# Pacing the context's chain: more of it beside block 1's feed-forward, fewer steps beside the causal attention

## The chip, the cores and the metric

The kernel runs on one core of one Trainium2 chip. The metric is the device time of one execution in microseconds (us). Its engines are TensorE (PE; PEld is its weight load), VectorE (DVE), ScalarE (ACT), GpSimd (POOL) and SyncE (SP), which issues most of the DMAs.

## What is computed

Two blocks of two layers each on 256 tokens of width 1024. The first has an RWKV time mix, a dense feed-forward, a causal attention ("moba": with 256 tokens there is one block of keys, so it is plain causal attention with 16 heads of 64) and a mixture of eight experts. The second works on the result x and on a context of its own, 256 tokens that don't depend on the first block.

```python
def first_block(x, ...):
    h = deepnorm_residual(x, rwkv7_time_mix(x), ln_g[0, 0], ln_b[0, 0])
    h = deepnorm_residual(h, swiglu(h), ln_g[0, 1], ln_b[0, 1])
    h = deepnorm_residual(h, moba_attention(h), ln_g[1, 0], ln_b[1, 0])
    return deepnorm_residual(h, moe_swiglu(h), ln_g[1, 1], ln_b[1, 1])

def second_block(x, ctx):                      # layer 0, the context's side:
    hc = modulate(rms_norm(xc, norm_g[0, 0]), csh1, csc1)
    yx, yc = even_mixer(hx, hc, ...)           # attention | bidirectional mLSTM, then w_out
    xc = xc + cg1 * rms_norm(yc, norm_g[0, 1])
    hc = modulate(rms_norm(xc, norm_g[0, 2]), csh2, csc2)
    xc = xc + cg2 * rms_norm(conv_ffn(hc, ...), norm_g[0, 3])
```

## The kernel before

All matrix products with large weights are made from float32 numbers split in two parts of a shorter format: each weight tile of 128 x 1024 is loaded by SP's queue (`wload`, L363) into one of six buffers `wraw`, copied by ACT into its high part `whi` (L303, pieces of 512 columns) and subtracted by DVE into its low part `wlo` (L306), with four buffers each. A product then takes three matmuls: high times high, low times high, high times low (L318). Transposes are matmuls too (L338). PSUM is two pools of four banks, `ps(0)` and `ps(1)`, for two chains of work.

Block 1's parts are generators, and so is the context's side of the second block, `ctx_even`. A step of a generator ends at a `yield`. `rated` runs a main chain and, after each of its steps, as many steps of the side chain as are due: a main step that yields nothing adds `rate`, one that yields a number adds that number, and the whole part of the sum is run. `block1_front` does this for four parts with the rates `A_RATES`: the time mix's output projection (`rwkv_out`), the feed-forward (`ffn_dense`), the causal attention (`moba`) and the router (`moe_route`). Within `moba`, `paced` lets the steps of the input projections yield `SIDE["moba_in"]` = 0, those of the softmax pipeline `SIDE["moba"]`, and those of the output projection `SIDE["moba_out"]` = 0; its first step (transposes of h) and its last (the norm) take the rate. What is still left of the side chain is run at the end.

Steps of the main chains: `rwkv_out` 5 (four of `lin_tok`, one of the norm); `ffn_dense` 36 (one of transposes; parts of 12 and 10 hidden tiles with 12 and 10 steps of up and gate products and six of the down projection each; one of the norm); `moba` one, then its input projections, ten of the softmax pipeline (eight pairs of heads: in step i the scores of pair i, the values of pair i - 2, the transposes of pair i - 1, the softmax of pair i), its output projection, and one of the norm.

Steps of `ctx_even`: one of the first norm, 15 of `even_proj`, 12 of `mlstm`, ten of `attend` (eight half pairs, pipelined in the same way; the first also finishes the mLSTM's output), four of `lin_tok` within `out_proj` (columns 0 to 511 by two halves of the depth, then columns 512 to 1023, both halves, by two halves of the tokens; the third also makes the gate's row), one of the residual, and one of the second norm (`modulated`, with 16 transposes and their splits).

The generators give the program order. A list scheduler of the language then puts each engine's instructions in order: program order is the priority, and of what is ready by its own model of time the earliest in the program goes first, so that a later instruction can slip ahead where an engine would be free.

Of the kernel before, what the change touches and what calls it, by code (L numbers as in the profile page):

```python
# [634 lines left out]

ADA_EVERY = 10
WKV_END = 286
A_RATES = (1.0, 0.8, 1.0, 0.0)
WKV_AR = 3
WKV_T = ((2.3, 1.0), (0.6, 1.7), (0.0, 1.0))  # L640
WKV_PC = (1, 0, 0)
# [348 lines left out]
def pipelined(n, scores, soft, turn, values):  # L990

    for i in range(n + 2):
        if i < n:
            scores(i)
        if i >= 2:
            values(i - 2)
        if 1 <= i <= n:
            turn(i - 1)
        if i < n:
            soft(i)  # L1000
        yield
# [31 lines left out]
def moba(N, st, ch=0):  # L1033
# [8 lines left out]
    def keep(dst):  # L1042
        def evac(c0, nt, p):
            k = c0 // P
            N.act(dst[:, k * T:(k + nt) * T].rearrange("p (n t) -> p n t", n=nt), p)
        return evac

    def vevac(c0, ncol, tb, p):
        N.act(v[:, tb * D + c0:tb * D + c0 + ncol], p[:, :ncol])
    yield from paced(chain(N.lin_T(ch, x, KD, a["moba_w_q"], D, keep(qT)), N.lin_T(ch, x, KD, a["moba_w_k"], D, keep(kT)),  # L1050
                           N.lin_tok(ch, x, KD, a["moba_w_v"], D, vevac)), SIDE["moba_in"])
    o = N.act_slots(2, 3, "oT")
# [40 lines left out]

    yield from paced(pipelined(8, scores, soft, turn, values), SIDE["moba"])

    def evac(c0, ncol, tb, p):
        q = h[:, tb * D + c0:tb * D + c0 + ncol]
        N.stt(q, q, ALPHA, p[:, :ncol], ALU.mult, ALU.add)
    yield from paced(N.lin_tok(ch, o, KD, a["moba_w_o"], D, evac, late=lambda: None), SIDE["moba_out"])
    N.layer_norm(lambda tb: h[:, tb * D:(tb + 1) * D], (1, 0), lambda tb: h[:, tb * D:(tb + 1) * D])  # L1100
# [487 lines left out]
def attend(N, ch, o, npr, nkb, score, vsrc, scale, biased, ch2=None):  # L1588

    nc = N.nc  # L1590
    ch2 = ch if ch2 is None else ch2
    nk = nkb * P
    sc, S, R, po = {}, {}, {}, {}

    def scores(i):
        sc[i] = [N.ps(ch) for _ in range(2)]
        for hh in range(2):
            score(i // 2, hh, i % 2, sc[i][hh])

    def soft(i):  # L1600
        S[i] = [N.t512("S")[:, :nk] for _ in range(2)]
        for hh in range(2):
            p, s = sc[i][hh][:, :nk], S[i][hh]
            if biased is not None:
                biased(i // 2, hh, i % 2, p, s)
                softmax_part(N, s, s, 1.0)
            else:
                softmax_part(N, s, p, scale)
        sc.pop(i)

    def turn(i):
        R[i] = turned(N, ch2, S.pop(i), nkb)

    def values(i):
        pr, qt = i // 2, i % 2
        if qt == 0:
            po[pr] = N.ps(ch2)
        for b in range(nkb):
            for hh in range(2):
                q = slice(hh * 64, hh * 64 + 64)  # L1620
                N.mm(po[pr][q, qt * P:(qt + 1) * P], vsrc(pr, hh, b), R[i][hh][:, b * P:(b + 1) * P], b == 0, b == nkb - 1)
        R.pop(i)
        if qt:
            out_split(N, o, pr, po.pop(pr))

    yield from pipelined(2 * npr, scores, soft, turn, values)
# [208 lines left out]
def mlstm_out(N, st, ch, E, o):  # L1835

    nc = N.nc
    hs = E["kh"][:, 1024:2048]
    og = E["qo"][:, 1024:2048]
    g = N.row_load(N.a["ev_ml_norm_g_2"][0])  # L1840
    N.tt(hs, hs, og, ALU.mult)
    h3 = hs.rearrange("p (n x) -> p n x", n=8)
    mu = N.sm(8, "mu")
    nc.vector.tensor_reduce(mu, h3, axis=AX.X, op=ALU.add)
    N.ts(mu, mu, 1.0 / 128)
    N.tt(h3, h3, bc(mu, 2, 128), ALU.subtract)
    N.act(og, hs, AF.Square)
    vr = N.sm(8, "vr")
    nc.vector.tensor_reduce(vr, og.rearrange("p (n x) -> p n x", n=8), axis=AX.X, op=ALU.add)
    rs = N.sm(8, "rs")  # L1850
    N.rpow(rs, vr, 8, 1.0 / 128, 1e-6)
    N.tt(h3, h3, bc(rs, 2, 128), ALU.mult)
    h2 = hs.rearrange("p (b x) -> p b x", b=2)
    N.tt(h2, h2, bc(g[:, :512], 1, 2), ALU.mult)
    for k in range(0, 4, 2):
        p = N.ps(ch)
        for i in range(2):
            for tb in range(2):
                N.tr(p[:, i * T + tb * P:i * T + (tb + 1) * P], h2[:, tb, (k + i) * P:(k + i + 1) * P])
        N.split(o.h[:, (4 + k) * T:(6 + k) * T], o.l[:, (4 + k) * T:(6 + k) * T], p)  # L1860
# [24 lines left out]
def even_x(N, st, ch, x, S):  # L1885
    nc, a, c = N.nc, N.a, N.c
    yield from even_proj(N, st, ch, x, S, "Ex")
    E, Ec = st["Ex"], st["Ec"]
    yield from paced(mlstm(N, st, ch, E, st["CT"], st["ms"], True), SIDE["mlstm"])

# [7 lines left out]
    mlstm_out(N, st, ch, E, o)  # L1898
    yield 8 * SIDE["bias"]
    qo, kv, kvc = E["qo"], E["kv"], Ec["kv"]  # L1900
# [12 lines left out]
    def biased(pr, hh, qt, p, S_):  # L1913
        h = 2 * pr + hh
        N.stt(S_[:, 0:T], p[:, 0:T], 0.125, bias[qt][:, h * T:(h + 1) * T], ALU.mult, ALU.add)
        N.act(S_[:, T:2 * T], p[:, T:2 * T], AF.Copy, scale=0.125)
    yield from paced(attend(N, ch, o, 4, 4, score, vsrc, 0.125, biased, ch2=1 - ch), SIDE["na"])
    st["yx_act"] = o
# [164 lines left out]
def ctx_even(N, st, ch=1):  # L2083

    a, nc = N.a, N.nc
    xc = N.slot(7, "xc")
    nc.scalar.dma_start(xc.rearrange("p (b c) -> p b c", b=2), a["ctx_2"][0].rearrange("(b p) c -> p b c", p=P))
    x = modulated(N, st, ch, xc, 0, 0, 1, (12, 13), N.slot(1, "cscr"))
    yield
    yield from even_ctx(N, st, ch, x, dict(qo=1, kv=11, ml=8, kh=9, h=(12, 13)))  # L2090
    yield from out_proj(N, st, ch, st["yc_act"], a["ev_w_out_2"], xc, 0, 1, 1)
    st["xc"] = xc
    st["cffn"] = modulated(N, st, ch, xc, 0, 1, 1, (8, 9), N.slot(1, "cscr2"))
    yield
# [8 lines left out]
    yield from mla_ctx(N, st, ch, x, (10, 11), 1, 9)  # L2103


SIDE = dict(moba_in=0, moba=1, moba_out=0, start=5, mlstm=1.25, bias=0.5, na=0.5, res0=3, end0=5, mla=1.5)


def x_chain(N, st, out, ch=0):
# [24 lines left out]
def chain(*gens):  # L2134
    for g in gens:
        yield from g
# [7 lines left out]
def paced(g, n):  # L2144
    for _ in g:
        yield n


def rated(main, side, rate):

    due = 0.0
    for n in main:
        due += rate if n is None else n
        advance(side, int(due))
        due -= int(due)


def block1_front(N, st):
# [8 lines left out]
    side = ctx_even(N, st)  # L2167
    for g, r in zip((rwkv_out, ffn_dense, moba, moe_route), A_RATES):
        rated(g(N, st), side, r)
# [26 lines left out]
```

## Time and profile before

| | us |
|---|---|
| median of 3 runs | 2859.82 |
| lowest, highest | 2858.45, 2868.52 |
| the profiled execution | 2855.15 |
| its span, first to last instruction | 2853.3 |
| TensorE busy in the span | 2756.7 |
| VectorE busy | 2209.9 |
| ScalarE busy | 1775.3 |
| GpSimd busy | 68.8 |

Matmuls are pipelined and their ends are modelled: two that follow each other overlap in the rows, so what one costs is read from the distance of the starts. Busy times are unions. A name such as `ps<-whi,ych` gives what is written and what is read, without buffer numbers. The names by which the chains are told apart: `h1T` the feed-forward's input, `hid` its hidden tiles, `h2T` the input of the causal attention, `kTm`, `qT` and `vm` its keys, queries and values, `oTh` and `oTl` its output; `nq_mlo` and `nk_nav` the context's queries, keys and values, `ych` and `ycl` its attention's output, which the context's output projection reads, `xc` the context, `cscr` its second norm. Both attentions write `S` and `R`; the causal one has 384 columns, or rows of 128 and 256, the context's 256. `consts` in the sum of S is the causal mask, `diag,consts` the gate's row.

### The profile page before, as it was taken

Reading aid. Unit: us, or ns where it says so; the run is one execution under the profiler, and the core shown is the slowest. Engines: PE = TensorE matmul, PEld = TensorE weight load, DVE = VectorE, ACT = ScalarE, POOL = GpSimd, SP = SyncE. Lnnn points to the kernel's source line nnn. Section 1 sums busy time; section 2 is a strip of 40 time slices with the busy share of each in tenths; the row PEclk is TensorE's granted clock in tenths of the full one; section 3 lists DMA queues with packets and bytes.
Section 4 is the critical chain, followed back from the end, with each engine's and each line's share of the span. In section 5 each row is a group of like instructions: output and inputs, shape, how many; then the busy total and the mean of one; then the engine's idle time right before and its main releaser. Section 6 shows DMA issues by size and latency. Waiting matters only on the chain. (4 is left out here: it accounts for less than half of the span.)

```text
span 2853.3 us, 49934 instructions
## 1 busy us (share of the span) xinstructions
PE 2756.7 (97%) x18356; PEld 2265.0 (79%) x18356; DVE 2209.9 (77%) x4350; ACT 1775.3 (62%) x3603; POOL 68.8 (2%) x87
## 2 busy tenths in 40 slices
PE   8999899999999999999999999999989999999898
PEld 8677589897866787778777777778877899877897
DVE  7356385577577989998998899987688787876767
ACT  5223265444566787787878878766547665666654
POOL 0011100000000000000000000000000000000000
PEclk9999999999999999999999999999999999999999
DMA  7444655544428999999999999975543455421453
GB/s 253 155 146 153 219 195 179 179 142 132 158 94 322 362 335 345 354 358 330 350 361 342 347 347 363 352 274 178 162 131 125 138 195 178 151 80 43 148 186 125
DMA packets 183663, 641.16 MB, mean 225 GB/s; under 512 B 22737, under 2 KB 28241, under 8 KB 183410
## 3 DMA queue, kind: packets, MB, share of 16 engines
q1 hardware_dynamic: 175200, 625.58, 63.2%
q10 hardware_dynamic: 8210, 12.30, 1.4%
q8 instruction: 146, 2.39, 0.3%
q14 instruction: 107, 0.88, 0.1%
HBM read 636.76 MB, written 1.05 MB: 224 GB/s over the span
## 5 line engine op out<-in xcount | busy, mean ns | idle before, releaser
L306 DVE TENSOR_TENSOR wlo<-wraw,whi 128x512 fp32r<-128x512 f32 (+1 forms) x2181 | 1375.8, 685 | 311.4 <-ACT whi L303 249.9
L303 ACT ACTIVATE whi<-wraw 128x512 fp32r<-128x512 f32 (+1 forms) x2181 | 1214.2, 621 | 408.9 <-PE ps L318 322.0
L318 PE MATMUL ps<-whi,xg 128*128 128x512 f32 x1792 | 497.4, 397 | 1.6 <-ACT whi L303 1.6
L318 PEld LDWEIGHTS ps<-whi,xg 128*128 128x128 f32 x1792 | 327.3, 188 | 83.6 <-ACT whi L303 23.3
L318 PE MATMUL ps<-wlo,xg 128*128 128x512 f32 x896 | 294.9, 400 | 0.4
L318 PE MATMUL ps<-whi,hT 128*128 128x512 f32 x896 | 260.2, 400 | 0.0
L318 PE MATMUL ps<-hT0h,whi 128*128 128x256 f32 (+2 forms) x872 | 216.2, 286 | 4.0 <-ACT whi L303 3.5
L318 PE MATMUL ps<-hT0l,whi 128*128 128x256 f32 (+2 forms) x872 | 216.1, 285 | 0.1
L318 PEld LDWEIGHTS ps<-wlo,xg 128*128 128x128 f32 x896 | 168.4, 188 | 54.1 <-DVE wlo L306 18.6
L318 PE MATMUL ps<-whi,hid 128*128 128x512 f32 x704 | 189.9, 405 | 9.9 <-DVE cv L315 6.7
L318 PEld LDWEIGHTS ps<-whi,hT 128*128 128x128 f32 x896 | 164.8, 189 | 31.8
L318 PEld LDWEIGHTS ps<-hT0h,whi 128*128 128x128 f32 (+2 forms) x872 | 167.8, 193 | 5.3 <-ACT whi L303 3.9
L318 PEld LDWEIGHTS ps<-hT0l,whi 128*128 128x128 f32 (+2 forms) x872 | 168.0, 193 | 0.9 <-DVE hT0l L306 0.4
L318 PE MATMUL ps<-wlo,hT 128*128 128x512 f32 x448 | 168.2, 415 | 0.0
L318 PEld LDWEIGHTS ps<-whi,hid 128*128 128x128 f32 x704 | 131.7, 191 | 43.3 <-issue 14.1
L315 DVE SCALAR_TENSOR_TENSOR cv<-ps,vecs,cv 128x255 f32<-128x255 f32 x264 | 124.3, 479 | 12.3 <-ACT cv L303 11.0
L318 PE MATMUL ps<-hT1h,whi 128*128 128x256 f32 (+1 forms) x504 | 128.6, 292 | 1.7 <-ACT whi L303 1.7
L318 PE MATMUL ps<-hT0h,wlo 128*128 128x256 f32 (+2 forms) x872 | 125.9, 285 | 1.8 <-DVE wlo L306 1.6
L318 PE MATMUL ps<-hT1l,whi 128*128 128x256 f32 (+1 forms) x504 | 126.5, 287 | 0.0
L318 PEld LDWEIGHTS ps<-hT0h,wlo 128*128 128x128 f32 (+2 forms) x872 | 114.1, 192 | 3.8 <-DVE wlo L306 3.1
L318 PEld LDWEIGHTS ps<-wlo,hT 128*128 128x128 f32 x448 | 84.3, 188 | 30.5 <-DVE wlo L306 14.1
L318 PEld LDWEIGHTS ps<-hT1h,whi 128*128 128x128 f32 (+1 forms) x504 | 97.2, 193 | 4.0 <-ACT whi L303 2.6
(528 smaller groups left out, 4480.5 us busy)
## 6 DMA issues: line engine op xcount, KB each, us to landing
wraw<-moe_w_down SPq DMA_DIRECT2D x224, 512.0 KB, 5.6
wraw<-moe_w_gate SPq DMA_DIRECT2D x222, 512.0 KB, 5.2
wraw<-moe_w_up SPq DMA_DIRECT2D x222, 512.0 KB, 5.4
wraw<-ffn_up SPq DMA_DIRECT2D x132, 512.0 KB, 3.7
wraw<-ada_w SPq DMA_DIRECT2D x96, 512.0 KB, 4.6
wraw<-ffn_down SPq DMA_DIRECT2D x66, 512.0 KB, 3.7
wraw<-ffn_w_gate SPq DMA_DIRECT2D x22, 512.0 KB, 4.0
wraw<-ffn_w_up SPq DMA_DIRECT2D x22, 512.0 KB, 3.6
```

Source lines behind the costliest of these rows:

```text
L303: self.nc.scalar.activation(out, in_, f, **kw)
L306: (eng or self.nc.vector).tensor_tensor(out, x, y, op=op)
L315: (eng or self.nc.vector).scalar_tensor_tensor(out, x, s, y, op0=op0, op1=op1)
L318: self.nc.tensor.matmul(out, l, r, start=start, stop=stop)
```

## The change

Two numbers. The rate of the side chain in the feed-forward goes from 0.8 to 1.0 steps a main step, and the pace in the causal attention's softmax pipeline from 1 to 0.75. No instruction is added or removed; the place of the context's steps in the program order changes, from the feed-forward's first main step on.

```diff
-A_RATES = (1.0, 0.8, 1.0, 0.0)
+A_RATES = (1.0, 1.0, 1.0, 0.0)
...
-SIDE = dict(moba_in=0, moba=1, moba_out=0, start=5, mlstm=1.25, bias=0.5, na=0.5, res0=3, end0=5, mla=1.5)
+SIDE = dict(moba_in=0, moba=0.75, moba_out=0, start=5, mlstm=1.25, bias=0.5, na=0.5, res0=3, end0=5, mla=1.5)
```

## Rows read from the trace of the kernel before

**Rows 1.** Busy us of each engine (and instructions) in four stretches, clock, DMA share, GB/s:
```profile
660.00:684.00 24.00, 23.75 (x125) 16.15 (x123) 19.60 (x55) 13.16 (x36) 0.00 (x0) 1.00 0.50 166
...
684.00:700.00 16.00, 10.96 (x53) 8.02 (x54) 14.58 (x35) 5.79 (x16) 2.96 (x2) 0.79 0.45 148
...
766.00:828.00 62.00, 56.74 (x330) 39.00 (x329) 46.73 (x157) 45.62 (x148) 0.00 (x0) 0.97 0.21 68
...
828.00:852.00 24.00, 22.97 (x109) 18.61 (x108) 21.84 (x48) 14.55 (x34) 3.50 (x5) 1.00 0.40 132
```

**Rows 2.** Timeline (start us, duration us, engine, line, operation): the context's chain, 660 to 793 us:
```profile
660.44 0.70 PE L318 MATMUL ps<-nk_nav,nq_mlo 64*128 64x256 f32 x4
...
698.11 0.47 ACT L303 ACTIVATE S<-ps,mx 128x256 f32<-128x256 f32 x1
...
767.07 0.66 PE L318 MATMUL ps<-R,nk_nav 128*64 128x128 f32 x8
...
792.05 0.77 PE L318 MATMUL ps<-whi,ych 128*128 128x512 f32 x1
```

**Rows 3.** TensorE's groups, 766 to 828.5 us: busy us, mean ns, idle before:
```profile
L318 PE MATMUL ps<-whi,ych 128*128 128x512 f32 x32 | 13.8, 430 | 0.0
...
L318 PE MATMUL ps<-diag,consts 128*128 128x512 f32 x4 | 1.9, 592 | 0.0
...
L318 PE MATMUL ps<-R,nk_nav 128*64 128x128 f32 x32 | 3.1, 285 | 0.0
...
L318 PE MATMUL ps<-nk_nav,nq_mlo 64*128 64x256 f32 x4 | 1.0, 428 | 0.0
...
L338 PE MATMUL ps<-ident,S 128*128 128x128 f32 x60 | 11.5, 299 | 4.7 <-DVE S L310 4.4 <-ACT ych L303 0.2
```

**Rows 4.** Timeline of TensorE: two starts of the context's output projection:
```profile
801.91 0.40 PE L318 MATMUL ps<-whi,ych 128*128 128x512 f32 x1
...
802.38 0.40 PE L318 MATMUL ps<-whi,ych 128*128 128x512 f32 x1
```

**Rows 5.** Timeline of TensorE at the first norm; waits stand in brackets:
```profile
684.23 0.44 PE L338 MATMUL ps<-ident,S 128*128 128x128 f32 x2 [0.47 <-ACT R L303]
...
690.68 0.44 PE L338 MATMUL ps<-ident,h 128*128 128x128 f32 x2 [1.03 <-DVE h L315]
...
694.75 1.54 PE L338 MATMUL ps<-ident,h 128*128 128x128 f32 x6 [2.97 <-DVE h L315]
```

**Rows 6.** Windows of 2 us; the granted clock is the third column from the right:
```profile
692.00:694.00 2.00, 0.00 (x0) 0.00 (x0) 1.86 (x5) 0.00 (x0) 1.45 (x1) 0.64 0.00 0
...
698.00:700.00 2.00, 2.00 (x14) 2.00 (x13) 1.65 (x6) 0.90 (x4) 0.00 (x0) 0.65 0.36 141
...
792.00:794.00 2.00, 2.00 (x7) 1.63 (x8) 0.75 (x4) 0.93 (x4) 0.00 (x0) 0.50 0.04 8
```

**Rows 7.** Window of the causal attention with hardly any neighbour, 782 to 792 us:
```profile
782.00:792.00 10.00, 5.88 (x35) 3.32 (x35) 6.95 (x28) 6.19 (x23) 0.00 (x0) 0.98 0.00 0
```

**Rows 8.** Timeline: starts of causal softmaxes, their transposes, the last output copy:
```profile
767.17 0.42 DVE L306 TENSOR_TENSOR S<-ps,consts 128x256 f32<-128x256 f32 x1
...
779.96 0.42 DVE L306 TENSOR_TENSOR S<-ps,consts 128x256 f32<-128x256 f32 x1
...
785.52 0.75 DVE L306 TENSOR_TENSOR S<-ps,consts 128x256 f32<-128x256 f32 x2
...
791.07 0.61 PE L338 MATMUL ps<-ident,S 128*128 128x128 f32 x3 [1.33 <-DVE S L310]
...
791.98 0.42 DVE L306 TENSOR_TENSOR S<-ps,consts 128x256 f32<-128x256 f32 x1
...
827.97 0.39 ACT L303 ACTIVATE oTh<-ps 128x256 fp32r<-128x256 f32 x1
```

**Rows 9.** VectorE's largest group, 828 to 852 us: weight splits:
```profile
L306 DVE TENSOR_TENSOR wlo<-wraw,whi 128x512 fp32r<-128x512 f32 x10 | 6.7, 683 | 0.0
```

**Rows 10.** Timeline of TensorE: transposes of the context's second norm:
```profile
839.56 0.63 PE L338 MATMUL ps<-ident,cscr 128*128 128x128 f32 x4 [0.86 <-DVE cscr L310]
```

## Prediction

> **What bounds the kernel now.** The change moves work of one chain (the context's) along another (block 1's), and both share the engines. So the first view is the busy time by stage [rows 1]: from 660 to 684 us (end of the feed-forward) and from 828 to 852 us (output projection of the causal attention) TensorE is busy nearly throughout. Between them lie two places where it isn't: the norm after the feed-forward, 684 to 700 us, with 10.96 of 16 us and a mean granted clock of 0.79, and the causal attention, 766 to 828 us, with 56.74 of 62 us. The sum of the work is the same before and after; so the time moves by what TensorE idles, or runs at the lower clock, in these two places.
>
> The second view is the timeline around them, to see which step of the context's chain stands where. By the code the chain has 44 steps: 16 to the end of the projections, 12 of mLSTM (17 to 28), ten of attention (29 to 38), four of output projection (39 to 42), the residual (43) and the second norm (44). Five run beside the time mix's projection. The feed-forward has 36 main steps, and 36 x 0.8 = 28.8, so step 33 is the last one there; 34 comes at the attention's first main step, 35 to 44 beside its ten softmax steps. The trace agrees [rows 2]: the first context scores come at 660.44, the softmax of step 34 at 698.11, behind the norm, four value products remain from 767.07 on, and the output projection starts at 792.05.
>
> **What the change does by this count.** 5 + 36 = 41: the context's attention and three of the four steps of its output projection end within the feed-forward, the third in its last step, after the norm's instructions. Step 42 comes at the attention's first step, and 10 x 0.75 = 7.5 lets 43 and 44 go beside the second and third softmax steps. Seven softmax steps have nothing beside them. So of what the words say, the output projection is not beside the softmax: it lies around the first norm.
>
> **Terms of the sum**, in us of the path that sets the end, which is TensorE's except in the causal attention.
>
> (a) Work moved out of the causal attention's stretch into stages where TensorE is full. Output projection: 96 matmuls (32 of each of three forms; [rows 3] shows one), two starts every 0.47 [rows 4], so 96 x 0.235 = 22.6. Gate row: 1.9. Context attention: value products 3.1, scores 1.0, and 12 of the 60 transposes of S (eight causal pairs have 48), 12 / 60 x 11.5 = 2.3 [rows 3]. Sum **+30.9**. Their splits on ACT and DVE go along: 16 of each, beside a DVE busy 19.6 of 24 us [rows 1]. DVE is 82% busy there, so I take +1 for stalls, between 0 and 5. Eight weight loads also move on SP's queue, ahead of those of the causal queries' weights, into a stretch with a DMA share of 0.45 [rows 1], and the norm's two row loads on ACT's queue hold two of the six weight buffers meanwhile; four are left. Nothing for these.
>
> (b) The hole at the first norm. TensorE waits five times, 0.47 + 0.47 + 1.03 + 0.23 + 2.97 = 5.2 (three of the rows, with first and last, in [rows 5]), and four windows of 2 us from 692 on show a clock between 0.50 and 0.65 [rows 6], hence about 4.6 us of work at 1.2 instead of 2.4 GHz, 2.3 lost. After the change, 48 matmuls of steps 41 and 42 (11.3 us) and the gate row lie ready there. The hole should close: **-7**, between -7.5 and -2 (if their splits hold up the norm on DVE, busy 14.58 of 16 there).
>
> (c) The causal attention without its neighbour. It lasts from its first mask at 767.17 to the last copy of its output, 827.97 + 0.39 = 828.4, thus 61.2. Alone, it is not bound by an engine: from 782 to 792 nearly nothing else runs, and DVE has 6.95, ACT 6.19, PE 5.88 of 10 us [rows 7]. It is a ring: mask, maximum, exponent, sum, scaling of one pair, then its transposes, and the next pair's copy follows those on ACT. One turn took 6.46 (785.52 to 791.98) alone, and 5.56 (779.96 to 785.52) with the last of the context's attention beside it [rows 8]. So 7 x 6.0 + 5.6 for the last softmax (785.52 to the transposes at 791.07) + 3.0 from there to the copy = 50.6. Residual and second norm add at most 21.84 - 6.7 = 15.1 us of DVE work [rows 1, 9], with four powers on an idle POOL; DVE has 3 of 10 us free, so most of it fits: +3. Length 53.6: **-7.6**. The ends: 7 x 5.56 + 8.6 = 47.5, -13.7; and at 1.2 GHz throughout, some 1 us more a turn and no room for the norm, 66.8, +5.6.
>
> (d) The second norm's 16 transposes no longer stand in the output projection: two waits, 0.86 and 0.18, and some 1.7 of work (the first of two groups in [rows 10]), **-2.7**, at worst 0.
>
> (e) TensorE, free half the time, can start the causal output projection early: its first 24 matmuls need only pairs 0 to 3. Before, hardly any slipped in, since TensorE was full. 24 x 0.23 = **-5.5**; between 0 and -11 (the second half of the columns too).
>
> (f) Coming out of a thin stretch costs clock: at 792 to 794 it was 0.50 [rows 6], after a stretch in which TensorE was busy 5.88 of 10 us [rows 7]. It now happens at the start of the causal output projection: **+1.5**, between 0 and 3.
>
> Sum: 30.9 + 1 - 7 - 7.6 - 2.7 - 5.5 + 1.5 = **+10.6**. All ends together would give -4 and +42.
>
> A rule that speaks against the change: the Trainium skill, "Perfetto Trace Analysis", Optimization Strategy, advises interleaving stretches whose most contended engines differ. The change takes matmuls away from a softmax stretch; by that rule alone the whole of (a) less (c) would be lost, some +23, about the first rival's time below. The trace agrees in part only, because the norm's hole is such a stretch too, and the work goes there.
>
> The profiled execution took 2855.15 us, with a span of 2853.3; the median of three runs is 2859.82, so 4.7 above it. The sum is a difference, and I add it to the median: 2859.8 + 10.6 = 2870.
>
> **Rivals.** *The clock stays down through the lone attention* (slower). Place: pairs 2 to 7. The pairs' own TensorE work is about 62 - 5.3 of waits - 30.9 = 25 us, 3.1 a pair at the full clock; at 1.2 GHz transposes, value products and scores double, and half of that lies in the ring: 1.5 a turn, six turns, +9, with (e) at half: 2870 + 12 = 2882. It decides once the granted clock is 0.5 from the second lone pair on. For it: at the end of the only lone stretch of before the clock did fall [rows 6]. Against: over that stretch it was still 0.98 in the mean [rows 7]. Beside it, the Trainium skill, "TensorE: Matmul & The Clock Gate", Part 1, says that activity releases the throttle and idleness brings it back; by it the sum would be this rival's. The trace agrees at both holes [rows 6].
>
> *The scheduler fills the lone attention*: both halves of (e) and the short ring, 2870 - 5.5 - 6 = 2858. For it: the ring of 5.56 was seen; against: PSUM has four banks a pool, and scores take two.
>
> *The words hold and the count doesn't*: the output projection stands beside the softmax from its first step. Then only the 6.4 us of context attention move, and the length stays about 61 less some 4: 2862. Against: the four value products left at 767.07 fit the count exactly.
>
> **How the numbers follow.** Forecast (+4 to +14) 0.48; clock rival 0.34; filled attention 0.10; the words' count 0.05; 0.03 for a gain from something not seen. About 0.5%, or 14.3 us, is what a measurement can tell from no change: faster is under 2845.5, slower over 2874.1. Forecast, filled and words lie within, the clock rival mostly above. Faster 0.04, same 0.60, slower 0.36. Range 2857 to 2886: from the filled attention to the clock rival with stalls of (a) at their upper end.
>
> **What would show it.** Right: the context's first output matmul well before the causal queries' first; no wait over 1 us and no low clock between the last feed-forward matmul and these; softmax turns of 5.5 to 6.5 us; TensorE under 60% busy in the causal attention. Wrong: output matmuls of the context between the causal scores; turns under 5 us, or over 7.5; the causal queries' first matmul later by much more, or less, than 30.9 + 1 - 7 = 25 us.

## Result and profile after

| | before | after |
|---|---|---|
| median, us | 2858.69 | 2881.55 |
| lowest, highest | 2855.43, 2868.52 | 2878.41, 2883.91 |
| the profiled execution | 2855.15 | 2880.99 |
| its span | 2853.3 | 2879.2 |

The change makes the kernel slower: ratio 1.0080, 95% interval 1.0069 to 1.0092, 22.9 us by the medians. The time lies in the predicted range, but the sum gave +10.6 us, under half of it. One of the twelve executions of a later run, mix, took 4461.15 us at a mean granted clock of 0.554 and is left out of its ratio.

Where it went is read from landmarks in the two traces, start to start. First the stages of the kernel after: the stretch that was the hole at the first norm [rows 1], the causal attention, and what is left of its output projection (busy us of PE, PEld, DVE, ACT, POOL; then the granted clock, the DMA share, GB/s).

```profile
694.00:715.00 21.00, 21.00 (x97) 16.62 (x96) 15.97 (x28) 12.20 (x23) 1.45 (x1) 1.00 0.64 213
...
783.80:862.70 78.90, 57.19 (x232) 35.15 (x231) 49.68 (x156) 42.49 (x138) 2.48 (x4) 0.68 0.10 29
862.70:873.80 11.10, 11.10 (x54) 8.89 (x52) 8.74 (x15) 2.16 (x5) 1.46 (x1) 1.00 0.16 49
```

The hole is closed: TensorE is busy throughout, at the full clock. The attention is the loss: 78.9 us instead of 61.2, at a mean granted clock of 0.68. Its timeline on VectorE shows the start of each pair's softmax, and between them the residual (`xc`) and the scaling of the second norm (`cscr`); the last line is the last output copy, on ScalarE.

```profile
783.80 0.76 DVE L306 TENSOR_TENSOR S<-ps,consts 128x256 f32<-128x256 f32 x2 [2.22 <-PE ps L318]
789.19 0.75 DVE L306 TENSOR_TENSOR S<-ps,consts 128x256 f32<-128x256 f32 x2
...
801.89 1.41 DVE L315 SCALAR_TENSOR_TENSOR xc<-ypr,rs,xc 128x512 f32<-128x512 f32 x2 [0.44 <-POOL rs L349]
803.22 0.75 DVE L306 TENSOR_TENSOR S<-ps,consts 128x256 f32<-128x256 f32 x2
...
810.82 0.75 DVE L310 TENSOR_SCALAR cscr<-xc,rs 128x1024 f32<-128x1024 f32 x1 [0.66 <-POOL rs L349]
819.80 0.75 DVE L306 TENSOR_TENSOR S<-ps,consts 128x256 f32<-128x256 f32 x2
824.57 0.75 DVE L306 TENSOR_TENSOR S<-ps,consts 128x256 f32<-128x256 f32 x2
832.72 0.75 DVE L306 TENSOR_TENSOR S<-ps,consts 128x256 f32<-128x256 f32 x2
...
862.33 0.39 ACT L303 ACTIVATE oTh<-ps 128x256 fp32r<-128x256 f32 x1 [0.99 <-PE ps L318]
```

With two more starts, 840.85 and 851.85, the turns are 5.4, 14.0 (residual), 16.6 (second norm), 4.8, 8.15, 8.1 and 11.0, and 10.9 to the last copy; the sum took 6.0 for each. In windows of 4 us the granted clock is 0.50 in most of this stretch:

```profile
784.00:788.00 4.00, 2.16 (x14) 1.19 (x11) 3.56 (x12) 2.44 (x11) 0.00 (x0) 1.00 0.23 62
...
800.00:804.00 4.00, 0.00 (x0) 0.00 (x1) 3.55 (x10) 0.28 (x1) 0.86 (x1) 0.50 0.00 0
...
828.00:832.00 4.00, 3.45 (x14) 2.21 (x12) 2.29 (x10) 2.40 (x10) 0.00 (x0) 0.50 0.00 0
```

The landmarks, before and after: first causal query matmul 697.23 and 714.91 (+17.7); from there to the first softmax 69.9 and 68.9 (-1.1); attention 61.2 and 78.9 (+17.7); from its end to the last causal output matmul's end 24.0 and 11.1 (-12.9). That is +21.4. The remaining 4.5 us of the spans' 25.9 lie in the mixture of experts and the second block; from the first expert matmul to the end, the traces of all kernels here scatter between 1967.8 and 1973.4 us, so I don't read them as an effect. (The changed kernel, busy and rate_only stand at the top of this scatter; change_order, which has the same steps in the same places as the changed kernel, stands at 1970.0.)

### The profile page after: what moved, and what is told of

The parts are those of the page before. It is cut to its first block, busy times and chain, and to the rows that moved or that the text cites. A ratio compares the mean times of both kernels' runs of the same rounds, so it can differ in the third digit from the quotient of the medians.

```text
span 2879.2 us, 49934 instructions
## 1 busy us (share of the span) xinstructions
PE 2774.1 (96%) x18356; PEld 2272.7 (79%) x18356; DVE 2213.0 (77%) x4350; ACT 1774.7 (62%) x3603; POOL 68.3 (2%) x87
```

## Two causes to tell apart, and a third

Two theories stood at first for the longer attention. *Blocks*: residual and second norm are runs of ScalarE and VectorE work that the pairs queue behind. *Clock*: with no context matmuls, TensorE falls to 1.2 GHz, and its work stands in the pairs' ring. The first three runs cross the two. Each ratio is taken against runs of the kernel before on the same chip, whose medians were 2854.93 to 2858.96 us. Lengths are read from the one profiled execution of each run, which lies up to 9 us from the run's median (rate_only 8.7 above, norm_early 7.3 below).

**norm_early** moves residual and norm ahead of the pairs (steps 43 and 44 at the attention's first step):

```diff
-A_RATES = (1.0, 1.0, 1.0, 0.0)
+A_RATES = (1.0, 1.0, 3.0, 0.0)
-SIDE = dict(moba_in=0, moba=0.75, ...
+SIDE = dict(moba_in=0, moba=0, ...
```

> The changed kernel, but the residual and second norm of the context (steps 43 and 44) are taken out of the causal attention: they follow step 42 at the attention's first main step, beside the causal queries' projection; nothing stands beside the softmax. Theory A (only the clock stretches the attention, turns of 8.1 us; the residual and norm cost what was forecast, 3 us): the attention shortens from 78.9 us by about 3, time 2878. Theory B (these two steps stand as blocks in the ring of the softmax, whose two turns around them took 14.0 and 16.6 us instead of 8): the attention takes about 7 x 8.1 + 11 = 68 us, and the time is 2866, between 2863 and 2870.

Measured: 2873.79 us, ratio 1.0063 (1.0050 to 1.0076); attention 67.8 us. No turn is over 12 us now, but the lone ones take 8.1. The attention is Theory B's; the time lies above its 2863 to 2870. Of the 11.1 us that the attention lost, 3.6 came back ahead of it, where residual and norm now stand (72.5 us from the first query matmul to the first softmax, instead of 68.9), and the single times lie apart: 2866.44, which is the profiled one, and 2868.68, then 2873.79 to 2874.39. One lone turn on TensorE:

```profile
814.94 1.32 PE L338 MATMUL ps<-ident,S 128*128 128x128 f32 x4 [0.55 <-DVE S L310]
816.39 1.11 PE L318 MATMUL ps<-R,vm 128*64 128x256 f32 x2
817.44 0.69 PE L338 MATMUL ps<-ident,S 128*128 128x128 f32 x2
818.71 1.54 PE L318 MATMUL ps<-R,vm 128*64 128x256 f32 x6 [0.58 <-ACT R L303]
820.18 2.35 PE L318 MATMUL ps<-kTm,qT 64*128 64x128 f32 x8
```

**busy** is the changed kernel with six matmuls behind each pair's scores whose results aren't used:

```diff
+        dm = N.ps(ch)
+        for _ in range(6):
+            N.mm(dm[:, 0:T], kT[:, pr * T:pr * T + P], qT[:, pr * T:(pr + 1) * T], True, True)
```

> The changed kernel with six idle matmuls (float32, 128x128 weights, 256 columns, result unused) behind the scores of each of the eight pairs, so that TensorE stays busy in the lone attention. Theory A (the 1.2 GHz clock stretches a turn from about 6 to 8.1 us): the granted clock stays at 1.00 in most of the attention, turns away from the residual and norm take 6 to 6.6 us though work is added, and the time falls by 8 to 12 us, to 2870 to 2874. Rival (the turn is bound by the ring on ACT and DVE, the clock does not matter): turns stay at 8 us or longer, time 2881 to 2892.

Measured: 2871.83 us, ratio 1.0061 (1.0049 to 1.0073); attention 68.0. The residual's and the norm's turns still take 12.7 and 16.6 us, the others 5.3 to 5.8 but for one of 8.3. Up to the last causal output matmul the gain is 4.7 us and not the 10.9 of the attention, because only 24 of these matmuls, instead of 48, stand before the attention's end.

**norm_early_busy** is both.

> Both edits at once: residual and norm out of the attention, six idle matmuls per pair in it. If A and B hold and add up: turns of 6 to 6.5 us at clock 1.00, an attention of 52 to 56 us, and a time of 2853 to 2860, about that of the kernel before. If the two overlap (the clock fell only because the residual and norm held up the scores): no better than the residual and norm out alone.

Measured: 2854.88 us, ratio 1.0002 (0.9993 to 1.0011), the time of before; attention 47.2, shorter than I expected, turns of 5.27 us, granted clock 1.00. TensorE is busy throughout it (47.15 us), idle matmuls included. So each cause alone looked like some 11 us of attention, and both together like 32. But the idle matmuls had done a second thing, which the rows of this run show:

```profile
810.81 2.86 PE L318 MATMUL ps<-qT,kTm 128*128 128x256 f32 x12
813.60 0.87 PE L318 MATMUL ps<-R,vm 128*64 128x256 f32 x8
814.40 0.77 PE L338 MATMUL ps<-ident,S 128*128 128x128 f32 x5
```

Here the value products (`R,vm`) of one pair come in one piece, and the transposes (`ident,S`) of the next follow. In norm_early transposes and value products are in pieces between each other, because both belong to one pair: the scores had slipped ahead of the transposes, and each piece waits for ScalarE's copy of the piece before. With the idle matmuls the scheduler kept the program's order; that it did so because TensorE looked full to its model is my reading and not shown. The next three runs are about the order.

**busy2** is norm_early with two idle matmuls a pair instead of six (`range(2)`). Its written order is norm_early's.

> The second norm early as in norm_early (residual and norm at the attention's first step), with two idle fp32 matmuls behind each pair's scores instead of six (norm_early_busy) or none (norm_early). Their results are not used. Theory: it is the clock that the idle matmuls bring back, so with a third of them the clock is either up, and the time that of norm_early_busy or some us less (2849 to 2856), or down, and the time that of norm_early (2870 to 2876), with little between. Rival (the idle matmuls help by their place in the order and not by the clock, in proportion to their number): turns of about 7.2 us and 2866 to 2869.

Measured: 2864.18 us, ratio 1.0021 (1.0011 to 1.0031); attention 57.4. The interleaved order at the full clock, beside norm_early at half:

```profile
792.00:812.00 20.00, 15.22 (x80) 8.15 (x79) 12.81 (x48) 11.09 (x40) 0.00 (x0) 1.00 0.01 3
```

```profile
800.00:832.00 32.00, 26.98 (x87) 14.34 (x87) 15.77 (x59) 13.89 (x52) 0.00 (x0) 0.50 0.00 1
```

Turns of 6.48 us (starts 792.41, 798.89, 805.38), against 8.14. I had expected a clock either up or down and the time of the one or the other run; the clock is up, and the time lies between. In this order the clock is worth 1.66 us a turn. From 6.48 to the 5.27 of norm_early_busy is then the order, or a little less than what it is worth, since there six idle matmuls a pair fill TensorE.

**norm_early_order** is norm_early with no matmul added and TensorE's order in the ring bound to the program's (`keep` is called for every matmul and transpose of the ring):

```diff
+    def keep(self, i):
+        if self.pin:
+            if self.last is not None:
+                self.tc.add_manual_dep(i.ins, self.last, NOSYNC, reason="ring order")
+            self.last = i.ins.name
```

> norm_early with TensorE's written order in the softmax ring bound to the program's: scores of pair i, value products of i - 2, transposes of i - 1. No matmul is added. The idle matmuls of norm_early_busy had two effects at once: the granted clock went from 0.50 to 1.00, and the scheduler wrote this order, where in norm_early and busy2 it wrote the transposes and value products of the same pair into each other, behind the scores two pairs ahead. busy2, with norm_early's order at a clock of 1.00, had turns of 6.48 us; norm_early 8.14 at 0.50; norm_early_busy 5.27. Theory (the order carries most): the value products' copy leaves the loop of the softmax, turns of 4.7 to 5.6 us even where the clock is 0.50; attention 43 to 50 us, time 2847 to 2857. Rival (the clock carries most): the clock stays at 0.50 and the turns are 6.8 to 8 us, time 2865 to 2873.

Measured: 2857.79 us, ratio 1.0004 (0.9995 to 1.0013); attention 50.0, turns of 5.2 to 6.0, at or a little above my theory's upper ends. (Its line numbers are a few higher than in the other kernels.) Three starts, TensorE's value products of the first turn and its rows of the second, and the window of six turns:

```profile
804.04 0.75 DVE L308 TENSOR_TENSOR S<-ps,consts 128x256 f32<-128x256 f32 x2
...
809.22 0.75 DVE L308 TENSOR_TENSOR S<-ps,consts 128x256 f32<-128x256 f32 x2
...
815.17 0.75 DVE L308 TENSOR_TENSOR S<-ps,consts 128x256 f32<-128x256 f32 x2
```

```profile
805.48 0.87 PE L326 MATMUL ps<-R,vm 128*64 128x256 f32 x8
...
809.19 0.92 PE L346 MATMUL ps<-ident,S 128*128 128x128 f32 x3 [0.47 <-DVE S L312]
810.04 1.66 PE L326 MATMUL ps<-kTm,qT 64*128 64x128 f32 x8
811.63 1.55 PE L326 MATMUL ps<-R,vm 128*64 128x256 f32 x8
813.48 0.92 PE L346 MATMUL ps<-ident,S 128*128 128x128 f32 x3 [0.30 <-DVE S L312]
```

```profile
793.00:826.00 33.00, 26.88 (x140) 14.99 (x140) 24.37 (x90) 20.89 (x79) 0.00 (x0) 0.71 0.00 1
```

In the second turn the value products take 1.55 us, as at the half clock (the granted clock from 809.22 to 815.17 is 0.50), yet the turn is 5.95: in this order they are beside the softmax and not in its loop. The turn before it, at 0.97, takes 5.18. So at the half clock the order is worth 2.2 us a turn (8.14 to 5.95), at the full one 1.3 (6.48 to 5.18), and in the bound order the clock is worth no more than 0.8 (another turn at 0.50, from 792.92, takes 5.50). ScalarE shows the same. Its copy of the attention's output waits for TensorE between the two heads' scores in norm_early, and stands between two exponents, without a wait, here:

```profile
810.02 0.49 ACT L303 ACTIVATE R<-ps 128x384 f32<-128x384 f32 x1 [1.82 <-PE ps L338]
810.41 0.27 ACT L303 ACTIVATE S<-ps 128x128 f32<-128x128 f32 x1
812.14 0.38 ACT L303 ACTIVATE oTh<-ps 128x256 fp32r<-128x256 f32 x1 [1.46 <-PE ps L318]
812.43 0.27 ACT L303 ACTIVATE S<-ps 128x128 f32<-128x128 f32 x1
```

```profile
806.80 0.49 ACT L305 ACTIVATE S<-S,mx 128x256 f32<-128x256 f32 x1
807.19 0.19 ACT L305 ACTIVATION_READ_ACCUMULATOR S<-S,mx 128x1 f32 x1
807.29 0.36 ACT L305 ACTIVATE oTh<-ps 128x256 fp32r<-128x256 f32 x1
```

So at least half of what the clock costs a turn, 1.66 us, goes when the interleaved order goes. The order alone suffices to get the time of before back, without added work; the clock alone, in busy2, does not quite (1.0021).

**change_order** is the changed kernel with the order bound, and nothing else.

> The changed kernel with the same order bound in the softmax ring, and nothing else. Theory (order, and the blocks of the residual and the second norm by themselves): the four late turns of 8.1 to 11 us fall to about 5.3, those with the residual (14.0) and the norm (16.6) stay over 10 us each; attention 62 to 70 us, time 2864 to 2873. Rival (the clock): all turns as before, 2878 to 2884.

Measured: 2870.15 us, ratio 1.0051 (1.0037 to 1.0065); attention 68.2. Only the turns with the blocks are long, 11.8 and 16.4 us (starts 788.59, 800.40, 816.78); the next four take 4.8, 6.0, 5.2 and 6.0. TensorE in the second:

```profile
807.23 1.08 PE L346 MATMUL ps<-ident,cscr 128*128 128x128 f32 x4 [11.97 <-DVE ss L308]
808.80 2.82 PE L346 MATMUL ps<-ident,cscr 128*128 128x128 f32 x12 [0.49 <-DVE cscr L312]
812.20 0.87 PE L326 MATMUL ps<-R,vm 128*64 128x256 f32 x8 [0.58 <-DVE tT L314]
813.38 1.14 PE L346 MATMUL ps<-ident,S 128*128 128x128 f32 x6 [0.31 <-DVE tT L314]
```

This pair's scores are scaled by 804.8, but TensorE's order has the norm's 16 transposes and the value products first, and the pair's own transposes come at 813.38; the next mask then stands behind the norm's last split on VectorE and starts at 816.78. A block costs its place in the engines' orders, not its share of VectorE. Of the 28.9 us between the attention of the changed kernel and that of norm_early_order, the order alone takes 10.7 (78.9 to 68.2), the blocks alone 11.1 (78.9 to 67.8); 7.1 go only when both are gone. Up to the last causal output matmul the order alone gains 9.0 us, the blocks alone 8.4, and both 23.0.

**rate_only** keeps the rate of the change and takes back the pace (0.75 to 1), so that the blocks come beside pairs 0 and 1.

> The feed-forward's rate is the changed kernel's (1.0), the pace beside the softmax that of before (1): steps 1 to 41 and 42 stand as in the changed kernel, the residual and the second norm come beside softmax steps 0 and 1 instead of 1 and 2. Theory (two causes, TensorE thin at 1.2 GHz and the two blocks of ScalarE and VectorE work in the ring): both are there as in the changed kernel, so the attention stays 75 to 80 us long and the time 2876 to 2885. Rival (the pace matters: where the blocks stand among the pairs sets what they cost): one block falls on the first pair, when TensorE is still at the full clock; if that saves most of it, the attention falls under 70 us and the time under 2873.

Measured: 2879.95 us, ratio 1.0069 (1.0055 to 1.0084); attention 79.3 (in an execution of 2888.66 us, whose surplus lies ahead: its first query matmul comes at 722.45, 7.5 us after the changed kernel's). At this rate the pace, 0.75 or 1, is not what matters. The pace alone was not tried.

**words** does what the change's words say, with the output projection beside the softmax: rate 0.9, pace 0.75, so that 38 steps are through before the pairs.

> The changed kernel with a rate of 0.9 instead of 1.0 in the feed-forward: 32 steps there, so the context's attention ends with step 38 at the causal attention's first main step, its output projection (39 to 42) stands beside softmax steps 1, 2, 3 and 5, residual and norm beside 6 and 7. This is what the words of the change describe. My rival for it gave 2862. If the place of the output projection decides (it keeps TensorE busy and the clock up): 2855 to 2864, no measurable difference from the kernel before. If instead the hole at the first norm decides (it is open again here): 2870 or more.

Measured: 2859.18 us, ratio 1.0017 (1.0009 to 1.0026), where the third rival had +2.2 us. Its attention lasts 79.0 us (770.12 to 849.08), as long as the changed kernel's, but at a granted clock of 0.96 and with the context's output projection and 78 of the 95 causal output matmuls of its trace in it; the last of these ends at 853.40, 1.0 us later than before. A long attention is a loss only as far as TensorE's other work isn't done in it. **spread** (0.9, 0.65) and **mix** (0.97, 0.4: 40 steps before the pairs, the last two of the projection spread among them) look for a better one.

> The feed-forward's rate is 0.9 and the pace beside the softmax 0.65: step 37 is the last beside the feed-forward, 38 comes at the attention's first step, 39 beside softmax step 1, 40 at 3, 41 at 4, the residual at 6 or 7, the second norm at 8 or 9. In the run with 0.9 and 0.75 (label words) TensorE stood nearly full until the output projection was through, and then the residual and norm fell into a lone, slow attention. Theory: work for TensorE between the pairs for longer keeps the clock up, and the two blocks come near the end, where the causal output projection fills in; attention 68 to 76 us, with the output projection of the context in it, time 2850 to 2858, at or below before. Rival (only the sum of TensorE's work counts and the blocks cost their full length wherever they stand): 2857 to 2863, as label words.

> The feed-forward's rate is 0.97 and the pace beside the softmax 0.4: 39 steps by the end of the feed-forward, 40 at the attention's first step, 41 and 42 (the last of the output projection) beside softmax steps 2 and 4, the residual at 7, the second norm at 9. So the hole at the norm is filled as in the changed kernel by two or so steps of matmuls, and the attention keeps half of the output projection, spread thin. Theory (clock and blocks): 24 matmuls spread over five pairs leave TensorE thin, so the clock falls all the same and the turns are 7 to 8 us with two long blocks late; attention 70 to 76 us, time 2862 to 2872. Rival (a few matmuls between the pairs are enough to keep the clock up): turns of 5.3 to 6.5 us, attention 58 to 66, time 2850 to 2858.

Measured: spread 2854.87 us, ratio 0.9989 (0.9980 to 0.9997), attention 64.1, shorter than I expected, granted clock 0.97 in it; mix 2856.06 us, ratio 0.9991 (0.9979 to 1.0002), attention 64.9 at 0.87. Time and attention of mix are in its rival's ranges and not in my theory's, though its turns, 4.6 to 11.4 us, are in neither: half of the output projection was enough to hide most of it. spread is the best found, by some 3 us, too little to build on.

**before_order** and **spread_order** bind the order in the kernel before and in spread.

> The kernel before with the same order bound in the softmax ring. Theory: two or three turns of before stood in the interleaved order (6.46 us for the one at 785.52); with the order bound they take about 5.3, and the output projection that fills the rest is as it was: 0 to 4 us less, 2854 to 2859. If the binding holds context matmuls up where TensorE is full, 0 to 4 us more.

> spread (rate 0.9, pace 0.65) with the same order bound in the softmax ring. Theory: spread's attention took 64.1 us with six steps of the context's chain beside it; the order shortens the turns that are not full of context matmuls by 1 to 3 us each, in three or four of them: attention 56 to 62, time 2846 to 2853. Rival (TensorE sets the turns here): as spread, 2853 to 2857.

Measured: 2856.22 us, ratio 1.0002 (0.9993 to 1.0011), with an attention of 58.9 instead of 61.2; and 2859.64 us, ratio 1.0008 (0.9998 to 1.0018), attention 65.8 instead of 64.1. Where TensorE is full, the bound order gains nothing; in spread my expectation was wrong, and the intervals of spread and spread_order don't meet, so binding cost some 5 us there. By the landmarks 1.3 us are lost up to the first query matmul, 1.7 in the attention and 2.5 in the rest of the output projection; the cause stays open.

## Why the prediction was right and wrong

The range held because the clock rival set its upper end. The sum, +10.6 for a measured +22.9, was as near as that only because its errors are of both signs: (c) was 25.3 us too low, (a) and (b) 7.2 and (d) to (f) 6.2 too high. By the prediction's own signs its account of the attention was wrong: turns over 7.5 us, TensorE busy 57.19 of 78.9 us (72%) where it had under 60%, the first query matmul 17.7 us later where it had 25.

**(a) and (b), forecast +24.9, measured +17.7.** The moved steps arrive where the count put them: the first query matmul follows the last of `ych` without a wait. Four traces differ only in how many steps they have through by then, and so price them:

| kernel | steps through | first query matmul |
|---|---|---|
| before | 34 | 697.23 |
| words | 38 | 699.79 |
| mix | 40 | 702.89 |
| after | 42 | 714.91 |

The rest of the attention cost 2.6 us where the terms have 6.4, half of the output projection 3.1 where they have 11.3, and the last two steps 12.0 where they have 13.2 (words, spread and spread_order, with equal counts, have it at 699.79, 701.02 and 702.32, so the small ones are rough). So the hole and its sides took in about 13 us (30.9 less 17.7) and not the 7 that I counted from waits and half-clock work [rows 5, 6]. Whether the hole was larger or the moved steps cheaper than their rows isn't settled. Once the place is full, moved matmuls cost nearly their full price.

**(c), forecast -7.6, measured +17.7: the step that failed.** By its parts: the five turns without a block, 37.4 us, against 30 (+7.4); the two with a block, 30.6, against 12 + 3 (+15.6); the end, 10.9 against 8.6 (+2.3).

The ring turn was mis-sized by a wrong reading of [rows 8]. I took 5.56 and 6.46 us for the same ring with and without a neighbour, and their middle for the turn. TensorE's timeline of before shows two orders:

```profile
780.06 0.66 PE L338 MATMUL ps<-ident,S 128*128 128x128 f32 x4
780.64 0.87 PE L318 MATMUL ps<-R,vm 128*64 128x256 f32 x8
...
785.72 0.65 PE L318 MATMUL ps<-R,vm 128*64 128x256 f32 x2
786.29 0.44 PE L338 MATMUL ps<-ident,S 128*128 128x128 f32 x2
787.31 0.87 PE L318 MATMUL ps<-R,vm 128*64 128x256 f32 x6 [0.58 <-ACT R L303]
```

The first has the value products in one piece, the second the interleaved order, which the change brings about for most of the lone pairs. The 6.46 agree with busy2's 6.48, and at 1.2 GHz they become 8.14.

The blocks were sized by VectorE's free share, three of ten us [rows 7]. A block in the ring costs about its whole length, waits included. The residual's rows on VectorE run from 796.57 to 803.30, 6.7 us, and the norm's from 808.09 to 819.88, 11.8; with the order bound, a turn with the residual takes 11.8 us and one with the norm 16.4, against 5.2 to 6.0, thus about 6 and 11 more. The rows show why: in the written order of each engine, ScalarE's four squares stand ahead of the copy that the value products need, VectorE's residual stands ahead of the next mask, whose scores start on TensorE at 792.75 and take 2.36 us (the mask starts at 803.22), and TensorE waits for the pair after that.

```profile
797.61 0.61 ACT L303 ACTIVATE sq<-ypr 128x512 f32<-128x512 f32 x1
798.13 0.19 ACT L303 ACTIVATION_READ_ACCUMULATOR sq<-ypr 128x1 f32 x1
798.22 0.84 ACT L303 ACTIVATE R<-ps 128x384 f32<-128x384 f32 x2
```

```profile
804.00 2.04 PE L318 MATMUL ps<-kTm,qT 64*128 64x128 f32 x8 [6.59 <-ACT S L303]
810.05 1.09 PE L338 MATMUL ps<-ident,cscr 128*128 128x128 f32 x4 [4.02 <-DVE ss L306]
```

Two smaller things in the prediction's working. The upper end of (c), 66.8, doesn't follow from its terms: a turn 1 us longer gives 57.6 before the norm; it also takes 1 us a turn for the clock, where the clock rival takes 1.5. And eight of the ten pipeline steps, not seven, have nothing beside them; no term rests on that.

**(d), (e) and (f), forecast -6.7, measured -12.9** from the end of the attention to that of the projection. More than 24 matmuls slipped ahead: 48 matmuls of the causal output projection stand before 862.7, beside the last two pairs, and the clock was back at 1.00 before it. Part of this is a loan: the same matmuls lengthen those turns to 11 us.

**The rivals.** The clock rival gave 2882, and its price, 1.5 us a turn, is right in the interleaved order: 1.66. But its time agrees by luck: blocks (+15.6) that it did not have stand against a cheaper move (-7.2) and an earlier projection. And its price depends on the order: in the bound one it is 0.8 at most, as norm_early_order shows. That activity releases the throttle, as the Trainium skill, "TensorE: Matmul & The Clock Gate", Part 1, has it, holds in sign: with matmuls added the clock is 1.00 (busy2), without 0.50 (norm_early). By the Trainium skill's advice on interleaving ("Perfetto Trace Analysis", Optimization Strategy) the loss would be some +23, about the measured figure; but norm_early_order takes the same matmuls out of the softmax and loses nothing measurable, so the lost interleaving is not the cause. The words' rival, refuted by the count, was near once its count was built: +2.2 against 4.2 by the medians. That too is luck: it had an attention of about 61 us less some 4, where 79.0 were measured, and the causal output projection, for which it had no change, ended 4.3 us after the attention instead of 24.0.

## What to carry to other kernels

When the neighbour of a softmax ring goes, look at the order in which its engine's instructions are written, and not only at the engine's load: a list scheduler can pull the next step's work ahead and put a slow step into the loop. Binding the program's order took some 17 us off norm_early, by the ratios, and needed no added work; in spread, where TensorE had other work nearly throughout, it cost some 5. And read a longer stretch together with the work that moved into it: the attention of words is as long as the changed kernel's, and the kernel is hardly slower. Chains of ScalarE and VectorE work with TensorE work behind them belong outside such a ring, whatever free share those engines show. Two turns of different length in one trace are a question to be answered from the rows before they are averaged.

## What was not expected of the hardware

Idle matmuls made a kernel faster: 48 of them, six a pair, took norm_early from 2873.79 to 2854.88 us, by the clock and the order together (the bound order alone reaches 2857.79). And a stretch at 1.2 GHz looks busier than the same work at 2.4: TensorE's rows cover 26.98 of 32 us of norm_early at 0.50, and 15.22 of 20 in busy2 at 1.00, with more matmuls in each turn. A high busy share is then no sign that TensorE is near its limit; the granted clock has to be read beside it.
